# Low parts of weights on VectorE alone, and a three-tap convolution shared differently between ScalarE and VectorE

## The chip, the cores and the metric

The kernel runs on one core of a Trainium2 chip. The metric is the device time of one execution in microseconds (us). TensorE (PE in the profile) multiplies matrices, VectorE (DVE), ScalarE (ACT) and GpSimd (POOL) work element by element, and SyncE (SP) issues the transfers.

## The reference, cut to what matters

The model has two kinds of blocks, each of depth 2, on 256 tokens of 1024 channels. The first block is a SwiGLU feed-forward, a mixer (a gated spatial unit and top-k attention), a second SwiGLU feed-forward. The second block is a mixer (a gated delta rule and dilated attention) and a feed-forward with a causal convolution over three tokens:

```
def _causal_dwconv(x, w):
    K = w.shape[0]
    S = x.shape[1]
    xp = jnp.pad(x, ((0, 0), (K - 1, 0), (0, 0)))
    y = xp[:, 0:S] * w[0]
    for j in range(1, K):
        y = y + xp[:, j:j + S] * w[j]
    return y

def _conv_glu_ffn(h, ffn_up, ffn_conv, ffn_conv_bias, ffn_down):
    u = _causal_dwconv(h @ ffn_up, ffn_conv) + ffn_conv_bias
    gate, val = jnp.split(u, 2, axis=-1)
    return (jax.nn.gelu(gate, approximate=True) * val) @ ffn_down
```

All of it is fp32, and every product with a weight matrix is taken to better than the precision of one pass of TensorE.

## The kernel before

Activations lie with channels on the 128 partitions and 256 tokens along the free axis. Every weight matrix comes from HBM in slabs of 128 x 1024 fp32 (512 KB; some are 768 or 512 wide). `parts` makes two tiles of each slab: ScalarE copies `wraw` to `whi` in TensorE's rounded format, and `wlo` is the remainder, `wraw` minus `whi`. `mm3` then runs three passes over a slab: eight pairs of a product with `whi` and one with `wlo` against the high part of the activations, and eight products with `whi` against their low part, 24 matmuls of 128 x 256 for a slab of 1024. The three tiles of a slab turn over in four buffers each: the load of a new slab (issued by SyncE) waits until both readers of an old `wraw` are done, and a new `whi` or `wlo` waits until TensorE has finished the slab four back.

Before the change a low part is divided: GpSimd makes the last `pool_cols` columns (384 as a rule) and VectorE the rest. In the second mixer (`mixer2`) the plan gives 24 slabs of each layer to GpSimd whole: their entries have 1024 or no number of columns of their own, and the line with `FULL` sets it to the whole width.

The stages follow each other: for each layer `swiglu`, `mixer1`, `swiglu`; then for each layer `mixer2`, `conv_glu`. A feed-forward has 22 chunks of 128 hidden channels; a chunk takes two slabs (gate and value) and gives one PSUM bank of 128 x 512. In `conv_glu` each chunk is multiplied by the row scales (`t`), convolved (`y`: ScalarE multiplies by the last tap and adds the bias, VectorE adds the other two taps, two instructions for each half), run through Gelu (`s`), multiplied by the other half (`p`) and split into `hid`: high part on ScalarE, low part on GpSimd. The down projection then takes 22 x 24 matmuls.

In `mixer2` the program writes TensorE's order by hand: the delta rule's chain of small steps (`Delta`) runs with products of the projections between its steps as filler (`pump`). The chain begins with the decay rates on tiny tiles (`bt`, `xa`, `spe`, `spz`, `sps`, `dg`: 128 x 8 or 16), side by side with the convolution of the keys (`ct`, `kT`), all on VectorE; TensorE waits for `dg`. Later GpSimd masks `LT` and makes `dM`, and VectorE's `Tf` needs them.

Elsewhere a scheduler orders each engine's instructions when the program is built; on the chip each engine takes its own list in that order.

Of the kernel before, what the change touches and what calls it, by code (L numbers as in the profile page):

```python
# [7 lines left out]
F32 = mybir.dt.float32  # L8
R32 = mybir.dt.float32r
AF = mybir.ActivationFunctionType  # L10
OP = mybir.AluOpType
# [6 lines left out]
P = 128  # L18
T = 256
D = 1024  # L20
# [5 lines left out]
NEG = -1.0e30  # L26
TAKEN = -3.0e38
BANKS = {"mm": 3, "sm": 5}
FIRST_COLS = 384
POOL_COLS = 384  # L30
FULL = 34
X_ENG = ((ACT, ACT), (ACT, ACT))
XT_ENG = ((ACT, ACT), (ACT, ACT))
WARM = (0, 5, 3)
# [56 lines left out]
class Kernel:  # L91
# [9 lines left out]
    def run(self, stages=None):  # L101
        nc, I, cp = self.nc, self.I, self.cp
        stages = stages or STAGES
        first = [s for s in stages if s[0] not in ("final", "mixer2", "glu")]
        vec1 = self.load(cp, [P, 8 + 2 * V1], I["vec1"], "vec1")
        self.x, self.ahead = [], []
        self.before = self.latest = self.ready = self.later = None
        self.plan, self.made, self.queue, self.far = [], [], [], 0
        self.pool_cols = FIRST_COLS
        for d in range(KD):  # L110
            n = self.new_x()
            nc.sync.dma_start(n, I["x"][d])
            self.x.append(n)
            if d == 1 and stages[0] == ("ffn1", 0):
                self.ahead.append(self.raw(I["ffn1_gu"][0][0, 0], D, 2))
        if self.ahead:
            self.made.append(self.parts(None, D, 0, step=D // 2))
            self.ahead.append(self.raw(I["ffn1_gu"][0][0, 1], D))
            idle = self.sp.tile([P, T], F32, name="sq", bufs=5)
            nc.vector.memset(idle, 0.0)  # L120
            self.warm(10, idle)
        self.ident = self.load(cp, [P, P], I["ident"], "ident")
        self.ones = cp.tile([P, 1], F32, name="ones")
        nc.vector.memset(self.ones, 1.0)
        self.mhalf = cp.tile([P, 16], F32, name="mhalf")
        nc.vector.memset(self.mhalf, -0.5)
        with Pool(self.tc, name="const1", bufs=1) as cp:
            con = self.vec2 = None
            for n, (kind, l) in enumerate(first):
                if n == 1:  # L130
                    self.second_constants()
                v = vec1[:, 8 + V1 * l:8 + V1 * (l + 1)]
                if kind == "mixer1":
                    if con is None:
                        con = {n: self.load(cp, list(I[n].shape), I[n], n)
                               for n in ("cos1", "sin1", "causal0", "causal1")}
                        self.cos1, self.sin1 = con["cos1"], con["sin1"]
                        self.causal = [con["causal0"], con["causal1"]]
                    self.mixer1(l, v)
                else:  # L140
                    g = V_FFN1 if kind == "ffn1" else V_FFN2
                    self.swiglu(v[:, g:g + 8], I[kind + "_gu"][l], I[kind + "_down"][l])
        if self.vec2 is None:
            self.second_constants()
        self.pool_cols = POOL_COLS
        with Pool(self.tc, name="const2", bufs=1) as cp:
            con = {n: self.load(cp, list(I[n].shape), I[n], n)
                   for n in ("cos2", "sin2", "dil0", "dil1", "cum", "whole", "levels", "ident2")}
            self.cos2, self.sin2 = con["cos2"], con["sin2"]
            self.dilated = [con["dil0"], con["dil1"]]  # L150
            self.cum, self.whole, self.levels = con["cum"], con["whole"], con["levels"]
            self.ident2 = con["ident2"]
            rest = stages[len(first):]
            for n, (kind, l) in enumerate(rest):
                v = self.vec2[:, V2 * l:V2 * (l + 1)]
                g = None
                if n + 1 < len(rest):
                    c = V2 * rest[n + 1][1] + (V_PRE if rest[n + 1][0] == "mixer2" else V_PREF)
                    g = self.vec2[:, c:c + KD]
                if kind == "final":  # L160
                    self.between(vec1[:, :KD], g)
                elif kind == "mixer2":
                    self.mixer2(l, v, g)
                else:
                    self.conv_glu(v, I["up2"][l], I["down2"][l], g)
        for d in range(KD):
            nc.sync.dma_start(self.out[d], self.x[d])
# [52 lines left out]
            self.nc.sync.dma_start(raw[:, c:c + step], src[:, c:c + step])  # L220
        return raw

    def piece(self, src, n, pool_cols=None):

        if self.plan or self.made:
            while self.plan and len(self.made) < 3:
                self.made.append(self.parts(*self.plan.pop(0)))
            for p in self.plan[len(self.ahead):self.far]:
                self.ahead.append(self.raw(p[0], p[1]))
            return self.made.pop(0)  # L230
        return self.parts(src, n, pool_cols)

    def parts(self, src, n, pool_cols=None, tiles=None, step=None):
        nc = self.nc
        raw = self.ahead.pop(0) if self.ahead else self.raw(src, n)
        if tiles is None:
            hi = self.wp.tile([P, n], R32, name="whi", tag="whi", bufs=4)
            lo = self.wp.tile([P, n], R32, name="wlo", tag="wlo", bufs=4)
        else:
            hi, lo = tiles  # L240
        hf = hi.bitcast(F32)
        step = step or n
        for a in range(0, n, step):
            e = a + step
            self.act(hi[:, a:e], raw[:, a:e])
            c = e - min(step, self.pool_cols if pool_cols is None else pool_cols)
            if c > a:
                self.tt(lo[:, a:c], raw[:, a:c], hf[:, a:c], OP.subtract)
            if c < e:
                self.tt(lo[:, c:e], raw[:, c:e], hf[:, c:e], OP.subtract, nc.gpsimd)  # L250
        return hi, lo

    def mm3(self, ps, w, hs, start=True, stop=True, M=P):
# [271 lines left out]
    def conv_glu(self, vec, wup, wdown, following):  # L525
        nc = self.nc
# [3 lines left out]
        with Pool(self.tc, name="glu", bufs=2) as fp:  # L530
            hid = []
            for j in range(NF):
                if pss:
                    ps = pss.pop(0)
                else:
                    ps = self.bank([P, 2, T])
                    for s in range(2):
                        self.mm3(ps[:, s, :], self.piece(wup[j, s], D), hs)
                t = fp.tile([P, 2, T], F32, name="t")
                self.tt(t, ps, rb2)  # L540
                y = fp.tile([P, 2, T], F32, name="y")
                for s in range(2):
                    c = j + NF * s
                    tap = lambda i: vec[:, V_FC + 3 * c + i:V_FC + 3 * c + i + 1]
                    self.act(y[:, s, :], t[:, s, :], AF.Identity, scale=tap(2), bias=vec[:, V_FB + c:V_FB + c + 1])
                    for i in (1, 0):
                        sh = 2 - i
                        self.stt(y[:, s, sh:], t[:, s, :T - sh], tap(i), y[:, s, sh:], OP.mult, OP.add)
                a = fp.tile([P, T], F32, name="s")
                self.act(a, y[:, 0, :], AF.Gelu_apprx_tanh)  # L550
                p = fp.tile([P, T], F32, name="p")
                self.tt(p, a, y[:, 1, :])
                hid.append(self.split(fp, p, "hid", NF, nc.gpsimd))
            ys, acc = [], None
            for m in range(KD):
                ps = self.bank([P, T])
                for q in range(0, NF, KD):
                    e = min(q + KD, NF)
# [307 lines left out]
    def mixer2(self, l, vec, following):  # L866
# [3 lines left out]
        wo = I["w_out2"][l]  # L870
        half = lambda m, i: (wo[m, :, 512 * i:512 * i + 512], 512)
        first = {"q": 0, "v": 8, "z": 12, "Q": 16, "K": 20}
        self.plan = [(w[i], D, 512) for i in range(4, 8)]
        for c in ORDER:
            if c == "V":
                self.plan += [(I["w_in2_v"][l, i], D) for i in range(4)]
            else:
                self.plan += [(w[first[c] + i], D, 512 if c in "qvz" else None) for i in range(2)]
                first[c] += 2
        self.plan = [p if n < 4 or n >= 4 + FULL else p[:2] + (p[1],) for n, p in enumerate(self.plan)]  # L880
        self.plan += [half(m, 0) for m in range(KD)]
        with Pool(self.tc, name="mix2", bufs=1) as mp, self.tc.manual_schedule(engines={PE}):

# [55 lines left out]
            def tap(c, i):  # L939
                return vec[:, V_DNC + 4 * c + i:V_DNC + 4 * c + i + 1]  # L940
# [89 lines left out]
            def delta_part():  # L1030
                for m in range(KD):
                    w = self.piece(None, 0)

                    t = [mp.tile([P, 512], R32, name=n, tag="big", bufs=16) for n in ("obh", "obl")]
                    wob.append(self.parts(*half(m, 1), None, t))
                    yield from self.mm3_steps(part(m), w, oa, m % 2 == 0, False, shared=True)

            def attention_part(m, i):
# [498 lines left out]
```

## Time and profile before

| | |
|---|---|
| median of 3 runs | 2001.97 us (1999.31 to 2010.21) |
| the profiled execution | 2004.46 us, of which its span is 2002.8 us |
| busy, share of the span | PE 95%, DVE 66%, ACT 49%, POOL 61% |
| granted clock of TensorE, mean | 0.981 |

The span runs from the first to the last instruction of the profiled execution. PE's matmuls are pipelined and their ends are modelled, so a busy PE is read together with the number of matmuls in a stretch.

### The profile page before, as it was taken

To read this page: it belongs to the slowest core of one execution; us is meant where nothing else is said; L and a number is where in the kernel's file an instruction comes from. 1 tells how busy PE (TensorE), PEld (TensorE's weight loads), DVE (VectorE), ACT (ScalarE), POOL (GpSimd) and SP (SyncE) were. 2 spreads that over 40 slices of the span, in tenths; PEclk is the share of its full clock that TensorE was granted. 3 is DMA by queue.
4 is the path that set the end of the run, shared out by engine and by line. 5 is a ranking of instruction groups with operands and counts; after the bars stand their busy time and mean duration, and the time that the engine had idled before them with its cause. 6 is when DMAs were issued, how large, how long until landed. Compare 5 with 4: busy or idle time off the path is not lost. (4 is left out here: it accounts for less than half of the span.)

```text
span 2002.8 us, 40107 instructions
## 1 busy us (share of the span) xinstructions
PE 1894.3 (95%) x15468; PEld 1822.9 (91%) x15468; DVE 1321.7 (66%) x2270; ACT 988.0 (49%) x1698; POOL 1217.8 (61%) x957
## 2 busy tenths in 40 slices
PE   9999999899999999999999978999899979999988
PEld 8999889899999999899999977879888978789888
DVE  7665685866657755966776567457884484559862
ACT  5444436444445544455445534455554445455553
POOL 5556475655565665665566757565556767555555
PEclk9999999999999999999899989999999989999999
DMA  7566554555656666555566633142555332235553
GB/s 233 187 183 187 182 162 130 187 171 188 184 185 198 193 183 192 170 165 154 169 197 187 193 117 116 57 147 88 166 158 174 126 121 92 68 113 169 165 164 114
DMA packets 102511, 317.17 MB, mean 158 GB/s; under 512 B 13360, under 2 KB 20912, under 8 KB 102320
## 3 DMA queue, kind: packets, MB, share of 16 engines
q1 hardware_dynamic: 102320, 314.61, 50.1%
q8 instruction: 121, 1.98, 0.4%
q14 instruction: 70, 0.57, 0.1%
HBM read 309.58 MB, written 1.05 MB: 155 GB/s over the span
## 5 line engine op out<-in xcount | busy, mean ns | idle before, releaser
L202 POOL TENSOR_TENSOR wlo<-wraw,whi 128x384 fp32r<-128x384 f32 (+1 forms) x609 | 931.0, 1532 | 490.0 <-ACT whi L185 487.3
L263 PE MATMUL mm<-h,whi 128*128 128x256 f32 x6048 | 1085.4, 282 | 18.2 <-DVE h L374 5.2
L263 PEld LDWEIGHTS mm<-h,whi 128*128 128x128 f32 x6048 | 931.9, 190 | 29.4 <-issue 12.1
L185 ACT ACTIVATE whi<-wraw 128x1024 fp32r<-128x1024 f32 (+2 forms) x611 | 611.0, 1003 | 421.2 <-PE mm L263 125.5
L263 PE MATMUL mm<-h,wlo 128*128 128x256 f32 (+1 forms) x3024 | 731.5, 282 | 30.5 <-DVE wlo L202 24.4
L202 DVE TENSOR_TENSOR wlo<-wraw,whi 128x640 fp32r<-128x640 f32 (+3 forms) x563 | 487.8, 867 | 333.8 <-ACT whi L185 332.2
L263 PEld LDWEIGHTS mm<-h,wlo 128*128 128x128 f32 (+1 forms) x3024 | 574.8, 190 | 38.6 <-DVE wlo L202 31.6
L263 PE MATMUL mm<-hid,whi 128*128 128x256 f32 x2112 | 378.9, 282 | 6.9 <-ACT hid L185 6.1
L263 PEld LDWEIGHTS mm<-hid,whi 128*128 128x128 f32 x2112 | 326.4, 190 | 7.7 <-ACT hid L185 6.5
L263 PE MATMUL mm<-hid,wlo 128*128 128x256 f32 x1056 | 257.3, 281 | 2.9 <-DVE wlo L202 2.9
L263 PEld LDWEIGHTS mm<-hid,wlo 128*128 128x128 f32 x1056 | 199.5, 189 | 4.1 <-DVE wlo L202 4.1
L185 ACT ACTIVATE hid<-p 128x256 fp32r<-128x256 f32 x132 | 55.1, 418 | 182.9 <-DVE p L202 182.8
L205 DVE SCALAR_TENSOR_TENSOR y<-t,vec,y 128x254 f32<-128x254 f32 (+1 forms) x176 | 135.8, 828 | 0.0
L202 DVE TENSOR_TENSOR p<-s,t 128x256 f32<-128x256 f32 x88 | 103.4, 1175 | 2.2 <-ACT s L185 2.2
L202 DVE TENSOR_TENSOR t<-mm,rb 128x512 f32<-128x512 f32 x132 | 90.5, 686 | 20.4 <-PE mm L263 12.2
L202 POOL TENSOR_TENSOR hid<-p,hid 128x256 fp32r<-128x256 f32 x44 | 34.7, 789 | 88.3 <-ACT hid L185 88.3
L202 DVE TENSOR_TENSOR hid<-p,hid 128x256 fp32r<-128x256 f32 x88 | 40.7, 463 | 40.2 <-ACT hid L185 40.2
L202 POOL TENSOR_TENSOR ssum<-ssum,sq 128x256 f32<-128x256 f32 x50 | 49.0, 981 | 12.1 <-ACT sq L185 11.1
L185 ACT ACTIVATE s<-y 128x256 f32<-128x256 f32 x44 | 18.4, 417 | 69.1 <-DVE y L205 68.9
L263 PE MATMUL mm<-zh,whi 128*128 128x256 f32 x256 | 46.6, 283 | 4.6 <-DVE gate L202 1.8
L205 DVE SCALAR_TENSOR_TENSOR h<-x,vec,h 128x256 fp32r<-128x256 f32 x72 | 45.8, 644 | 6.2 <-ACT h L185 5.1
L185 ACT ACTIVATE y<-t,vec 128x256 f32<-128x256 f32 x88 | 47.5, 589 | 1.7 <-DVE t L202 1.7
(296 smaller groups left out, 2038.4 us busy)
## 6 DMA issues: line engine op xcount, KB each, us to landing
wraw<-ffn_gu_in SPq DMA_DIRECT2D x175, 512.0 KB
wraw<-w_in_a_in SPq DMA_DIRECT2D x112, 512.0 KB
wraw<-up_in SPq DMA_DIRECT2D x88, 512.0 KB
wraw<-ffn_down_in SPq DMA_DIRECT2D x64, 512.0 KB
wraw<-down_in SPq DMA_DIRECT2D x32, 512.0 KB
wraw<-ffn_down_in SPq DMA_DIRECT2D x32, 384.0 KB
wraw<-w_in_v_in SPq DMA_DIRECT2D x16, 512.0 KB
wraw<-w_out_in SPq DMA_DIRECT2D x16, 512.0 KB
```

What stands on the lines that cost most here:

```text
L185: return self.nc.scalar.activation(out, in_, func, **k)
L202: return (eng or self.nc.vector).tensor_tensor(out, a, b, op=op)
L205: return self.nc.vector.scalar_tensor_tensor(out, a, s, b, op0=op0, op1=op1)
L263: mm = lambda a, b, **f: self.nc.tensor.matmul(ps, a, b, skip_group_check=shared, **f)
```

## The change

Low parts are made by VectorE alone, in one instruction for a whole slab; the columns' counts and the plan's numbers go. In `conv_glu` ScalarE multiplies by the middle tap into a new tile `m` (one instruction for each half), VectorE still adds the first tap for each half, and one VectorE instruction adds `m`, moved by one token, to both halves.

```
-FIRST_COLS = 384
-POOL_COLS = 384
-FULL = 34
...
         for a in range(0, n, step):
             e = a + step
             self.act(hi[:, a:e], raw[:, a:e])
-            c = e - min(step, self.pool_cols if pool_cols is None else pool_cols)
-            if c > a:
-                self.tt(lo[:, a:c], raw[:, a:c], hf[:, a:c], OP.subtract)
-            if c < e:
-                self.tt(lo[:, c:e], raw[:, c:e], hf[:, c:e], OP.subtract, nc.gpsimd)
+            self.tt(lo[:, a:e], raw[:, a:e], hf[:, a:e], OP.subtract)
         return hi, lo
...
                 y = fp.tile([P, 2, T], F32, name="y")
+                m = fp.tile([P, 2, T], F32, name="m")
                 for s in range(2):
                     c = j + NF * s
                     tap = lambda i: vec[:, V_FC + 3 * c + i:V_FC + 3 * c + i + 1]
                     self.act(y[:, s, :], t[:, s, :], AF.Identity, scale=tap(2), bias=vec[:, V_FB + c:V_FB + c + 1])
-                    for i in (1, 0):
-                        sh = 2 - i
-                        self.stt(y[:, s, sh:], t[:, s, :T - sh], tap(i), y[:, s, sh:], OP.mult, OP.add)
+                    self.act(m[:, s, :], t[:, s, :], scale=tap(1))
+                    self.stt(y[:, s, 2:], t[:, s, :T - 2], tap(0), y[:, s, 2:], OP.mult, OP.add)
+                self.tt(y[:, :, 1:], y[:, :, 1:], m[:, :, :T - 1], OP.add)
...
-        self.plan = [(w[i], D, 512) for i in range(4, 8)]
+        self.plan = [(w[i], D) for i in range(4, 8)]
...
-                self.plan += [(w[first[c] + i], D, 512 if c in "qvz" else None) for i in range(2)]
+                self.plan += [(w[first[c] + i], D) for i in range(2)]
                 first[c] += 2
-        self.plan = [p if n < 4 or n >= 4 + FULL else p[:2] + (p[1],) for n, p in enumerate(self.plan)]
```

VectorE in the steady part of the up projection of `conv_glu`, one chunk, before:

```order
L205 SCALAR_TENSOR_TENSOR y<-t,vec_2479,y 128x255 x2
L205 SCALAR_TENSOR_TENSOR y<-t,vec_2479,y 128x254 x2
L202 TENSOR_TENSOR wlo<-wraw,whi 128x640
L202 TENSOR_TENSOR p<-s,y 128x256
L202 TENSOR_TENSOR t<-mm,rb 128x512
L202 TENSOR_TENSOR wlo<-wraw,whi 128x640
```

The same chunk after the change (lines have moved up by five):

```order
L200 SCALAR_TENSOR_TENSOR y<-t,vec_2412,y 128x254 x2
L197 TENSOR_TENSOR y<-y,m 128x2x255
L197 TENSOR_TENSOR wlo<-wraw,whi 128x1024
L197 TENSOR_TENSOR p<-s,y 128x256
L197 TENSOR_TENSOR t<-mm,rb 128x512
L197 TENSOR_TENSOR wlo<-wraw,whi 128x1024
```

Of the four tap instructions two stay, one addition of both halves takes the place of the other two, and the low parts are whole slabs.

ScalarE in the same chunk, before:

```order
L185 ACTIVATE whi<-wraw 128x1024
L185 ACTIVATE s<-y 128x256
L185 ACTIVATE hid<-p 128x256
L185 ACTIVATE whi<-wraw 128x1024
L185 ACTIVATE y<-t,vec_2479 128x256 x2
```

ScalarE in the same chunk, after:

```order
L180 ACTIVATE whi<-wraw 128x1024
L180 ACTIVATE s<-y 128x256
L180 ACTIVATE whi<-wraw 128x1024
L180 ACTIVATE hid<-p 128x256
L180 ACTIVATE y<-t,vec_2412 128x256
L180 ACTIVATE m<-t,vec_2412 128x256
L180 ACTIVATE y<-t,vec_2412 128x256
L180 ACTIVATE m<-t,vec_2412 128x256
```

Two multiplications by the middle tap are new, and a copy of a slab now stands between Gelu and the high part of `hid`.

VectorE at the head of the delta rule in the second layer's `mixer2`, from the first decay rates to the first tap of the keys, before:

```order
L202 TENSOR_TENSOR bt<-sm,rt 128x32
L202 TENSOR_TENSOR bt<-bt 128x2x8
L202 TENSOR_TENSOR xa<-bt,dt 128x8
L205 SCALAR_TENSOR_TENSOR spe<-xa 128x8
L999 COPY rb<-sm 128x256
L202 TENSOR_TENSOR ct<-mm,rb 128x512
L1139 TENSOR_SCALAR spz<-spe 128x8
L1141 RECIPROCAL spz<-spz 128x8
L205 SCALAR_TENSOR_TENSOR kT<-ct,vec_2479,kT 128x255
```

The same place after the change:

```order
L197 TENSOR_TENSOR xa<-bt,dt 128x8
L197 TENSOR_TENSOR wlo<-wraw,whi 128x1024
L200 SCALAR_TENSOR_TENSOR spe<-xa 128x8
L989 COPY rb<-sm 128x256
L197 TENSOR_TENSOR wlo<-wraw,whi 128x1024
L197 TENSOR_TENSOR ct<-mm,rb 128x512
L197 TENSOR_TENSOR wlo<-wraw,whi 128x1024
L1129 TENSOR_SCALAR spz<-spe 128x8
L197 TENSOR_TENSOR wlo<-wraw,whi 128x1024
L1131 RECIPROCAL spz<-spz 128x8
L200 SCALAR_TENSOR_TENSOR kT<-ct,vec_2412,kT 128x255
L197 TENSOR_TENSOR wlo<-wraw,whi 128x1024
```

Five low parts that GpSimd made stand here among the decay rates, and a sixth follows before `dg`; in the first layer there are six as well. TensorE's own order of instructions is the same before and after.

## Rows read from the trace of the kernel before

**Rows 1.** The page's chain that ended last, by line.

```profile
PE mm L263 9%; DVE y L205 5%; DVE wlo L202 2%; ACT whi L185 2%; DVE p L202 1%; POOL wlo L202 1%; PE sm L1262 1%; PE sm L336 1%; POOL x L202 1%; PE sm L1388 1%; PE sm L1272 0%; ACT as L185 0%; PE sm L1387 0%; PE sm L263 0%; POOL ssum L202 0%
```

**Rows 2.** Stretches: length, busy (count) of PE, PEld, DVE, ACT, POOL; PEclk, DMA, GB/s.

```profile
589.79:710.63 120.84, 120.84 (x1067) 120.84 (x1067) 86.22 (x111) 60.25 (x88) 71.80 (x46) 1.00 0.61 191
...
1153.72:1362.94 209.22, 184.76 (x1460) 166.86 (x1458) 121.82 (x278) 97.42 (x236) 127.46 (x107) 0.95 0.32 104
1362.94:1517.00 154.06, 138.26 (x1151) 133.77 (x1151) 131.67 (x193) 90.56 (x151) 89.37 (x77) 1.00 0.47 149
...
1578.26:1782.50 204.24, 185.70 (x1459) 168.32 (x1459) 122.98 (x278) 100.40 (x247) 132.21 (x113) 0.96 0.30 98
1782.50:1936.00 153.50, 138.51 (x1150) 134.30 (x1150) 131.33 (x193) 90.36 (x151) 89.09 (x76) 1.00 0.46 150
```

**Rows 3.** Timeline of VectorE, one chunk of `conv_glu`: start, duration, instruction, [idle before].

```profile
1445.44 0.41 DVE L202 TENSOR_TENSOR p<-s,y 128x256 f32<-128x256 f32 x1
1445.77 0.68 DVE L202 TENSOR_TENSOR t<-mm,rb 128x512 f32<-128x512 f32 x1
1447.29 0.83 DVE L202 TENSOR_TENSOR wlo<-wraw,whi 128x640 fp32r<-128x640 f32 x1 [0.84 <-ACT whi L185]
1448.03 3.19 DVE L205 SCALAR_TENSOR_TENSOR y<-t,vec,y 128x255 f32<-128x255 f32 x4
1451.15 0.81 DVE L202 TENSOR_TENSOR wlo<-wraw,whi 128x640 fp32r<-128x640 f32 x1
1451.88 0.41 DVE L202 TENSOR_TENSOR p<-s,y 128x256 f32<-128x256 f32 x1
```

**Rows 4.** Timeline of ScalarE, the same chunk.

```profile
1445.88 0.42 ACT L185 ACTIVATE hid<-p 128x256 fp32r<-128x256 f32 x1 [0.98 <-DVE p L202]
1446.21 1.05 ACT L185 ACTIVATE whi<-wraw 128x1024 fp32r<-128x1024 f32 x1
1447.16 1.08 ACT L185 ACTIVATE y<-t,vec 128x256 f32<-128x256 f32 x2
1448.14 1.05 ACT L185 ACTIVATE whi<-wraw 128x1024 fp32r<-128x1024 f32 x1
```

**Rows 5.** Timeline of TensorE, the next chunk's first product with the low part.

```profile
1452.02 0.38 PE L263 MATMUL mm<-h,wlo 128*128 128x256 f32 x1 [0.72 <-DVE wlo L202]
```

**Rows 6.** Timeline of GpSimd, the same chunk's low part of `hid`.

```profile
1452.83 0.74 POOL L202 TENSOR_TENSOR hid<-p,hid 128x256 fp32r<-128x256 f32 x1 [2.27 <-ACT hid L185]
```

**Rows 7.** Timeline of VectorE at the head of the second layer's `mixer2`.

```profile
1593.81 2.08 DVE L202 TENSOR_TENSOR bt<-bt 128x16 f32<-128x16 f32 x1
...
1605.31 2.63 DVE L205 SCALAR_TENSOR_TENSOR kT<-ct,vec,kT 128x255 f32<-128x255 f32 x1
...
1608.14 0.48 DVE L205 SCALAR_TENSOR_TENSOR kT<-ct,vec,kT 128x254 f32<-128x254 f32 x1
...
1611.43 0.16 DVE L205 SCALAR_TENSOR_TENSOR dg<-sps,ea 128x8 f32<-128x8 f32 x1
```

**Rows 8.** Timeline of GpSimd in the same place.

```profile
1598.11 9.55 POOL L202 TENSOR_TENSOR wlo<-wraw,whi 128x1024 fp32r<-128x1024 f32 x4
```

**Rows 9.** TensorE's waits in the first layer's `mixer2`: total, times, longest.

```profile
PE sm L1171 <- DVE dg L205: 9.8, 1, 9.8
PE sm L1264 <- POOL LT L1244: 5.7, 1, 5.7
PE mm L263 <- POOL wlo L202: 2.6, 2, 2.1
```

**Rows 10.** TensorE's waits in the second layer's `mixer2`.

```profile
PE sm L1171 <- DVE dg L205: 7.5, 1, 7.5
PE sm L1274 <- DVE Tf L202: 3.5, 2, 3.2
PE mm L263 <- POOL wlo L202: 3.4, 3, 2.1
```

**Rows 11.** Groups by line and shape: low parts of whole slabs on GpSimd.

```profile
L202 POOL TENSOR_TENSOR wlo<-wraw,whi 128x1024 fp32r<-128x1024 f32 x48 | 116.3, 2435 | 61.6 <-ACT whi L185 61.5
```

More of the change, by code (lines that the diff above doesn't have):

```diff
@@ L108, in run @@
         self.plan, self.made, self.queue, self.far = [], [], [], 0
-        self.pool_cols = FIRST_COLS
         for d in range(KD):
@@ L116, in run @@
         if self.ahead:
-            self.made.append(self.parts(None, D, 0, step=D // 2))
+            self.made.append(self.parts(None, D, step=D // 2))
             self.ahead.append(self.raw(I["ffn1_gu"][0][0, 1], D))
@@ L144, in run @@
             self.second_constants()
-        self.pool_cols = POOL_COLS
         with Pool(self.tc, name="const2", bufs=1) as cp:
@@ L221, in raw, with piece @@
         return raw
-    def piece(self, src, n, pool_cols=None):
+    def piece(self, src, n):
         if self.plan or self.made:
@@ L230, in piece, with parts @@
             return self.made.pop(0)
-        return self.parts(src, n, pool_cols)
-    def parts(self, src, n, pool_cols=None, tiles=None, step=None):
-        nc = self.nc
+        return self.parts(src, n)
+    def parts(self, src, n, tiles=None, step=None):
         raw = self.ahead.pop(0) if self.ahead else self.raw(src, n)
@@ L1034, in delta_part @@
                     t = [mp.tile([P, 512], R32, name=n, tag="big", bufs=16) for n in ("obh", "obl")]
-                    wob.append(self.parts(*half(m, 1), None, t))
+                    wob.append(self.parts(*half(m, 1), t))
                     yield from self.mm3_steps(part(m), w, oa, m % 2 == 0, False, shared=True)
```

## The prediction

> **What bounds the kernel now.** I first read the chain that ended last. TensorE holds the largest share, and the largest share of another engine is VectorE's taps of the convolution, 5% of the span, with low parts and the copies of slabs behind them [rows 1]. So I looked for the stages in which TensorE does not run at its own pace. That pace comes from an up projection of `swiglu`: 1067 matmuls in 120.84 us with PE busy throughout, 0.1133 us each [rows 2]. There the weights, the low parts and the transfers keep up. A chunk of two slabs, 48 matmuls, needs 5.44 us at this pace.
>
> The up projection of `conv_glu` is slower. Its stretch takes 154.06 us with 1151 matmuls, which need 130.4 us, so 23.7 us are lost; in the second layer it is 153.50 us for 1150, 23.2 us lost [rows 2]. The timeline of VectorE shows why: from one `p` to the next, 1445.44 to 1451.88, is 6.44 us [rows 3]. The parts form a ring over two engines. `p` releases the high part of `hid` on ScalarE, behind it in ScalarE's list stands the copy of a slab, VectorE waits 0.84 us for this copy, makes a low part, runs the four taps (3.1 us), makes the other low part, and only then comes the next `p` [rows 3, 4]. TensorE meets the ring's end as a wait of 0.72 us for a low part, once a chunk [rows 5].
>
> The second place is `mixer2`, 209.22 and 204.24 us [rows 2]. Its largest waits of TensorE are those for `dg`, 9.8 and 7.5 us, then for the masked `LT` (5.7) or `Tf` (3.5) and for low parts of GpSimd (2.6 and 3.4) [rows 9, 10].
>
> **The price of VectorE's instructions.** The spacing of starts counts, since an instruction begins a little before the last has ended. A low part of 640 columns is spaced 0.74 us and `p` of 256 0.33 us [rows 3]. That is 1.07 ns a column, so a low part of 1024 is an estimated 1.15 us, and an instruction of 512, such as `t`, or of 510, such as the new addition, 0.60 us. A tap that nothing holds lasts 0.48 us [rows 7] and is spaced 0.40; in the steady chunk the four take 3.12 us, 0.78 each [rows 3]. The difference is GpSimd at work on low parts.
>
> **The change in `conv_glu`.** VectorE's list for a chunk is then 2 x 1.15 (low parts) + 0.60 (`t`) + 2 x 0.40 (first taps) + 0.60 (the addition) + 0.33 (`p`) = 4.63 us. GpSimd keeps one instruction per chunk, the low part of `hid`, 0.74 us [rows 6]; if it holds VectorE for all of that each time, 5.37. ScalarE's list is 2 x 0.95 (slabs), 0.98 (both `y`), at most 0.98 (both `m`, which have a scale and no bias) and 2 x 0.33 (`s` and the high part of `hid`), 4.52 us [rows 4]. All stay below 5.44. The ring opens as well: the copy no longer stands behind the high part of `hid`. What is left of it, from one addition to the next, is a low part 1.15, `p` 0.33, `t` 0.60, then ScalarE's four multiplications 1.96 and the addition with its hand-overs 0.65: 4.7 us. So TensorE should set the pace, with `t` waiting for it. Low parts are made about two chunks ahead and the buffers of `whi` come free at TensorE's pace, as they already do in `swiglu`, so its waits for them should go. The transfers are those of the fast stretch, which asked for 191 GB/s [rows 2].
>
> I leave 3 us of the loss at the head of each stage, where TensorE waits for the norm, and take 20.5 us a layer, **41 us** in all. Bounds: all of it, 47; and 22 if hand-overs and GpSimd's instruction keep a chunk at 5.9 us, since half of the 1.00 us per chunk is then lost again.
>
> **The change in `mixer2`.** At its head five of VectorE's small instructions, from `bt` to the second tap of the keys, last 2.08 to 2.63 us, 11.6 us together [rows 7]; unhindered, tiny ones take 0.16 and taps 0.48 [rows 7], 1.4 us together. The other 10.1 us are spent while GpSimd makes low parts, four of them in 9.55 us [rows 8], 2.44 each in the mean [rows 11].
>
> The Trainium skill, SBUF — State Buffer, section "Who interferes with whom", says that a VectorE instruction with two SBUF inputs and a GpSimd instruction that reads SBUF exclude each other, and that the later one blocks until the other has ended. By that rule the whole 10.1 us is blocking and goes with GpSimd's low parts, as in my sum; if the engines merely shared bandwidth, sixteen elements could hardly last 2.08 us and part of it would stay. The trace agrees with the rule.
>
> Against it stand six low parts that VectorE now makes ahead of `dg`, 6 x 1.15 = 6.9 us. The balance is 3.2 us; some of the new work falls into VectorE's waits for ScalarE, and the first layer has one more held instruction, so I take 4 us a layer, **8 us**. Bounds: nothing, if the low parts wait for ScalarE's copies in the middle of the chain, and 11.
>
> The waits for `LT`, `Tf` and GpSimd's low parts sum to 15.2 us [rows 9, 10]. GpSimd is then free when the mask comes. But TensorE's own order asks for the low parts of two more slabs before it turns `LT`, and VectorE makes them only behind its eight instructions for `LT`. I estimate a new wait of 2.5 us a layer from two such low parts (2 x 1.15), and take 15.2 - 5 = **10 us**. Bounds: 0 and 15.
>
> VectorE has room: in each `mixer2` it is busy 122 of over 204 us [rows 2], stalls included, and gains 24 low parts, 28 us, and the rest of the halved slabs of the output projection, some 6 us.
>
> **The clock.** In both `mixer2` stretches the granted clock is 0.95 and 0.96 in the mean, against 1.00 in the others shown [rows 2]; it is at 1.2 GHz for a part of them, after TensorE's long waits. At 209.22 and 204.24 us that is 10.5 and 8.2 us of lost clock. Shorter waits should return about a third, **6 us**; bounds 0 and 12.
>
> **Everything else.** `swiglu` is at TensorE's pace already; VectorE's list for its chunk, about 3.6 us by the prices above, is still below 5.44, so nothing comes or goes. At the joints, where VectorE makes norms and low parts by turns, blocking by GpSimd goes and wider low parts come; the first mixer has both too. I take **3 us** gain, bounds -8 and +8.
>
> **The sum.** 41 + 8 + 10 + 6 + 3 = 68 us. The profiled execution took 2004.46 us, 1.66 more than its span of 2002.8, and lies 2.49 above the median of 2001.97. 2002.8 - 68 = 1934.8, plus 1.66 is 1936.5; against the median of the runs, **1934 us**.
>
> **Rivals.**
> 1. `conv_glu` comes only to 5.9 us a chunk, by VectorE, GpSimd's `hid` and the hand-overs together. For it: 5.37 of 5.44 leaves little. Against it: `t` waits for TensorE anyway and GpSimd's work falls mostly there. It costs 19 us: 1953. Chance 10%.
> 2. `mixer2` gives nothing: low parts in front of the decay rates and of `Tf` cost what the blocking cost. For it: VectorE's list is one queue, and a low part that waits for ScalarE's copy, which waits for TensorE, holds all behind it. Then 8 + 10 + 6 us are not gained: 1958. Chance 10%. The Trainium skill, TensorE: Matmul & The Clock Gate, section "Architectural detail", says that VectorE takes its instructions strictly in order; no run here shows it yet with a low part at the front.
> 3. Slower than before: in each `mixer2` all that VectorE gains in work, 34 us, lands on the chain that TensorE waits for, and as much blocking is hidden as was before. That is +68 against 44 gained elsewhere: 2026. It decides when a `mixer2` grows by more than 22 us. Against it: VectorE is idle there for 80 us. Chance 3%.
> 4. The change does not do its work in `conv_glu`: ScalarE, with two multiplications more and copies that wait for TensorE to free a buffer, becomes the ring, and a chunk stays at 6.4. Only 27 us come: 1975. Against it: 4.52 us of work. Chance 3%.
>
> The forecast has the other 74%.
>
> **How the numbers follow.** The forecast's own range, with its terms' bounds combined, is 1912 to 1955. The 8-in-10 range takes in rivals 1 and 2 with their own spread and the case that all upper bounds come: 1910 to 1966. A measurement of this kernel can tell 0.5%, 10 us, from no change; below 1992 lie the forecast and rivals 1, 2 and 4. Faster 0.95, same 0.02, slower 0.03.
>
> **What would show it.** Right: spacing of `p` in `conv_glu` near 5.44 us and TensorE's wait for a low part gone there; taps at 0.48 us, low parts of 1024 at about 1.21; the small instructions before `dg` at 0.2 us or less, and waits for `dg` of 4 to 6 us; no wait for `LT` over 3 us. Wrong: a low part of 1024 far above 1.2 us, ScalarE idle in front of copies while VectorE waits behind them, or a wait of TensorE for VectorE in `mixer2` that is longer than before [rows 9, 10].

## The result and the profile after

The median is 1944.81 us (1940.72 to 1945.77, 4 runs), against 2003.73 us (1999.31 to 2010.21, 4 runs) of the kernel before on the same chip: a ratio of 0.970, with a 95% interval of 0.9668 to 0.9731. The forecast was 1934 us, with 1910 to 1966 as its range; the time came out 11 us above the one and inside the other. The profiled execution took 1945.77 us, its span is 1944.0 us.

The page's chain that ended last, by line, after the change (against [rows 1]):

```profile
PE mm L253 10%; PE sm L618 0%; PE sm L1378 0%; PE sm L1262 0%; PE sm L253 0%; PE mm L574 0%; PE sm L326 0%; PE sm L1377 0%; DVE yo L197 0%; PE sm L637 0%; PE mm L576 0%; PE mm L575 0%; POOL ssum L197 0%; PE sm L651 0%; POOL x L197 0%
```

The chain is followed back only to 1631.92 us here, so the two lists cover different stretches. Where it runs, from the second layer's `mixer2` on, it holds no tap of the convolution, two low parts and three copies of slabs, all in `mixer2`, and no line of another engine than TensorE reaches 1%.

Stretches of the kernel after, in the order of [rows 2]: `mixer2` and the up projection of `conv_glu`, first and second layer.

```profile
1144.27:1352.19 207.92, 187.18 (x1461) 168.95 (x1459) 126.97 (x303) 98.39 (x236) 48.06 (x61) 0.96 0.32 103
1352.19:1478.16 125.97, 124.88 (x1081) 124.45 (x1082) 115.43 (x164) 102.96 (x185) 37.98 (x30) 0.99 0.54 174
1544.94:1744.72 199.78, 185.98 (x1458) 168.72 (x1459) 126.81 (x302) 102.25 (x247) 57.53 (x69) 0.96 0.31 99
1744.72:1870.62 125.90, 124.83 (x1081) 124.39 (x1082) 115.49 (x164) 103.00 (x185) 38.01 (x30) 0.99 0.55 174
```

`mixer2` took 209.22 and 204.24 us before and hardly became shorter: 1.3 and 4.5 us. Where the gain lies is seen when the program is cut at the first matmul of each stage (the first that reads `h`, `hid` or `oa`, and the first of the attention's output) and the lengths are compared. The first row of `mixer2` is called its first part below. Cut so, the up projection before ends at 1502.57 us, and the last 14.4 us of the stretch of 154.06 us in [rows 2] already belong to the down projection.

| us from TensorE's first matmul of the stage to the next (the last one to VectorE's last instruction) | before | after | difference |
|---|---|---|---|
| six stages of the first block together | 1148.15 | 1138.44 | -9.7 |
| `mixer2`, to the output of the delta rule | 165.88, 161.25 | 159.27, 152.17 | -6.6, -9.1 |
| `mixer2`, attention's stretch | 23.95, 23.60 | 28.86, 28.11 | +4.9, +4.5 |
| `mixer2`, output and norm | 19.39, 19.39 | 19.79, 19.50 | +0.4, +0.1 |
| `conv_glu`, up projection | 139.63, 139.25 | 125.97, 125.90 | -13.7, -13.4 |
| `conv_glu`, down projection | 75.69, 78.14 | 66.78, 70.56 | -8.9, -7.6 |

VectorE in the steady part of `conv_glu`, one chunk (against [rows 3]):

```profile
1433.10 0.69 DVE L197 TENSOR_TENSOR y<-y,m 128x510 f32<-128x510 f32 x1
1433.71 1.22 DVE L197 TENSOR_TENSOR wlo<-wraw,whi 128x1024 fp32r<-128x1024 f32 x1
1434.84 0.42 DVE L197 TENSOR_TENSOR p<-s,y 128x256 f32<-128x256 f32 x1
1435.18 0.69 DVE L197 TENSOR_TENSOR t<-mm,rb 128x512 f32<-128x512 f32 x1
1435.93 1.23 DVE L197 TENSOR_TENSOR wlo<-wraw,whi 128x1024 fp32r<-128x1024 f32 x1
1437.08 1.36 DVE L200 SCALAR_TENSOR_TENSOR y<-t,vec,y 128x254 f32<-128x254 f32 x2
...
1440.28 0.42 DVE L197 TENSOR_TENSOR p<-s,y 128x256 f32<-128x256 f32 x1
```

From one `p` to the next is 5.44 us, to the hundredth the pace taken for TensorE; it was 6.44. ScalarE now waits for TensorE to free a buffer of `whi`, which says the same:

```profile
1434.84 1.07 ACT L180 ACTIVATE whi<-wraw 128x1024 fp32r<-128x1024 f32 x1 [0.59 <-PE mm L253]
```

GpSimd's one instruction in the chunk (against [rows 6]) became longer, 1.48 us instead of 0.74:

```profile
1436.28 1.48 POOL L197 TENSOR_TENSOR hid<-p,hid 128x256 fp32r<-128x256 f32 x1 [3.96 <-ACT hid L180]
```

It begins beside VectorE's low part of 1435.93 and ends at 1437.76. The first of the two taps, alone, lasts 0.96 us, twice the 0.48 of a free one [rows 7], and the second 0.47:

```profile
1437.08 0.96 DVE L200 SCALAR_TENSOR_TENSOR y<-t,vec,y 128x254 f32<-128x254 f32 x1
```

VectorE at the head of the second layer's `mixer2` (against [rows 7]):

```profile
1559.55 0.17 DVE L197 TENSOR_TENSOR bt<-bt 128x16 f32<-128x16 f32 x1
1559.76 0.17 DVE L197 TENSOR_TENSOR xa<-bt,dt 128x8 f32<-128x8 f32 x1
1559.85 1.22 DVE L197 TENSOR_TENSOR wlo<-wraw,whi 128x1024 fp32r<-128x1024 f32 x1
...
1568.00 0.48 DVE L200 SCALAR_TENSOR_TENSOR kT<-ct,vec,kT 128x255 f32<-128x255 f32 x1
```

The tiny instructions shown last 0.17 us instead of 2.08 and a tap 0.48 instead of 2.63, with low parts of 1.22 us between them. TensorE's waits in `mixer2` (against [rows 9, 10]), first layer:

```profile
PE sm L1161 <- DVE dg L200: 5.1, 1, 5.1
PE mm L253 <- DVE wlo L197: 4.5, 2, 3.7
PE sm L637 <- POOL as L197: 3.5, 1, 3.5
PE sm L1262 <- DVE Tf L197: 2.3, 5, 0.8
PE sm L1264 <- DVE Tf L197: 1.5, 2, 1.3
```

and second layer:

```profile
PE sm L1161 <- DVE dg L200: 5.4, 1, 5.4
PE sm L637 <- POOL as L197: 3.4, 1, 3.4
...
PE sm L1264 <- DVE Tf L197: 1.7, 2, 1.5
PE sm L1262 <- DVE Tf L197: 1.0, 3, 0.4
```

The waits for `LT` and for GpSimd's low parts are gone. New are a wait for a low part of VectorE (first layer only) and one for `as`, the probabilities of the attention, which was 0.2 us before in the first layer. The waits for `Tf` became longer in the first layer (3.8 us, 0.8 before). The low part of the first layer's longest wait, 3.7 us, stands in VectorE's list behind instructions on `x`, which finish the stage before:

```profile
1208.66 2.81 DVE L200 SCALAR_TENSOR_TENSOR x<-x,vec,sm 128x256 f32<-128x256 f32 x7
...
1212.07 1.21 DVE L197 TENSOR_TENSOR wlo<-wraw,whi 128x1024 fp32r<-128x1024 f32 x1
```

The wait for `as` has to do with ScalarE's order; runs 3 and 4 show how much. ScalarE at the start of the attention, before:

```profile
1320.38 1.28 ACT L185 ACT_TABLE_LOAD   x1
1322.92 0.51 ACT L185 ACTIVATE as<-as,ast 128x256 f32<-128x256 f32 x1 [1.26 <-DVE ast L631]
```

and after:

```profile
1306.80 0.64 ACT L180 ACTIVATE obh<-wraw 128x512 fp32r<-128x512 f32 x1 [2.21 <-DMA wraw<-w_out_in]
...
1309.29 0.64 ACT L180 ACTIVATE whi<-wraw 128x512 fp32r<-128x512 f32 x1 [1.32 <-issue]
1309.94 1.28 ACT L180 ACT_TABLE_LOAD   x1
1311.23 0.51 ACT L180 ACTIVATE as<-as,ast 128x256 f32<-128x256 f32 x1
```

Before, the load of the table for the exponential was done 1.26 us ahead of the scores. After, two more copies of slabs (and one more `obh`) stand in front of it. A copy lasts 0.6 us, but ScalarE stands idle ahead of them, 2.21 us until a slab's transfer has landed and 1.32 us more. So the load begins only at 1309.94, when VectorE had already written the maxima, `ast`, at 1308.77.

### The profile page after: what moved, and what is told of

It is laid out like the page before. It is cut to its first block, busy times and chain, and to the rows that moved or that the text cites. A ratio compares the mean times of both kernels' runs of the same rounds, so it can differ in the third digit from the quotient of the medians.

```text
span 1944.0 us, 38985 instructions
## 1 busy us (share of the span) xinstructions
PE 1880.5 (97%) x15468; PEld 1820.5 (94%) x15468; DVE 1336.7 (69%) x2274; ACT 1026.8 (53%) x1786; POOL 323.3 (17%) x332
## 5 line engine op out<-in xcount | busy, mean ns | idle before, releaser
L197 DVE TENSOR_TENSOR wlo<-wraw,whi 128x1024 fp32r<-128x1024 f32 (+2 forms) x611 | 715.8, 1174 | 370.9 <-ACT whi L180 368.6
L253 PE MATMUL mm<-hid,whi 128*128 128x256 f32 x2112 | 374.1, 279 | 0.0
L197 POOL TENSOR_TENSOR ssum<-sq 128x256 f32<-128x256 f32 x19 | 23.3, 1231 | 662.7 <-ACT sq L180 662.7
L197 POOL TENSOR_TENSOR hid<-p,hid 128x256 fp32r<-128x256 f32 x44 | 64.6, 1470 | 178.9 <-ACT hid L180 147.5
L197 POOL TENSOR_TENSOR ssum<-ssum,sq 128x256 f32<-128x256 f32 x50 | 54.9, 1099 | 203.9 <-ACT sq L180 178.4
L200 DVE SCALAR_TENSOR_TENSOR y<-t,vec,y 128x254 f32<-128x254 f32 x88 | 53.9, 652 | 0.3 <-ACT y L180 0.3
L197 POOL TENSOR_TENSOR as<-as,ast 128x512 f32<-128x512 f32 (+1 forms) x32 | 26.4, 827 | 124.4 <-DVE ast L626 94.9
L200 DVE SCALAR_TENSOR_TENSOR h<-x,vec,h 128x256 fp32r<-128x256 f32 x72 | 41.1, 578 | 6.0 <-ACT h L180 5.1
L180 ACT ACTIVATE m<-t,vec 128x256 f32<-128x256 f32 x88 | 43.3, 496 | 1.8 <-DVE t L197 1.8
L253 PEld LDWEIGHTS mm<-zh,whi 128*128 128x128 f32 x256 | 39.0, 188 | 2.4 <-ACT zh L180 2.4
```

What stands on the lines that cost most here:

```text
L180: return self.nc.scalar.activation(out, in_, func, **k)
L197: return (eng or self.nc.vector).tensor_tensor(out, a, b, op=op)
L200: return self.nc.vector.scalar_tensor_tensor(out, a, s, b, op0=op0, op1=op1)
L253: mm = lambda a, b, **f: self.nc.tensor.matmul(ps, a, b, skip_group_check=shared, **f)
```

## The experiments

Each time is a median, with the ratio to the kernel before on the same chip (2006.59, 2005.35 and 2005.23 us in the three groups of runs, in this order).

**1. The convolution alone.** The kernel before, with only the lines of `conv_glu` changed as in the change.

> The kernel before with the change's convolution alone; GpSimd keeps its share of the low parts. Theory (GpSimd's low parts hold VectorE, and both parts of the change are needed): the remaining taps still last about 0.8 us each and the addition over 1 us, so a chunk of conv_glu comes from 6.44 only to 5.7 to 6.0 us, the two up projections give back 20 to 30 of the 43.6 us, the rest of the kernel stays as before: about 1977 us. Rival (fewer instructions on VectorE are enough): a chunk at 5.44 us, both stages as after the change, about 1960 us. Under a second rival (the new convolution is worth nothing while GpSimd holds VectorE) a chunk stays above 6.2 us, 1995 us or more.

1974.56 us, 0.9839 (0.9817 to 0.986). One chunk on VectorE, and GpSimd beside it:

```profile
1441.01 1.25 DVE L202 TENSOR_TENSOR p<-s,y 128x256 f32<-128x256 f32 x1
...
1443.75 1.35 DVE L205 SCALAR_TENSOR_TENSOR y<-t,vec,y 128x254 f32<-128x254 f32 x2
...
1446.55 1.25 DVE L202 TENSOR_TENSOR p<-s,y 128x256 f32<-128x256 f32 x1
```
```profile
1440.29 2.84 POOL L202 TENSOR_TENSOR wlo<-wraw,whi 128x384 fp32r<-128x384 f32 x2 [1.40 <-ACT whi L185]
```

`p` lasts 1.25 us, held by GpSimd, where a free one lasts 0.42. Still the chunk is at 5.54 us, between the theory's 5.7 and the rival's 5.44. The up projection takes 125.97 us in the first layer, as after the whole change, and 128.65 in the second (at the slower pace of TensorE that run 5 shows). The 0.1 us by which a chunk is late is met by TensorE at the start of the first layer's down projection, as a wait of 2.8 us for `hid`, and the down projections keep 71.58 and 71.59 us. So for the up projection the rival is right. Run 1 gained 32 of the 59 us; the others are not the convolution's alone.

**2. The low parts alone.** The kernel after, with the four old taps.

```
-                    self.act(m[:, s, :], t[:, s, :], scale=tap(1))
-                    self.stt(y[:, s, 2:], t[:, s, :T - 2], tap(0), y[:, s, 2:], OP.mult, OP.add)
-                self.tt(y[:, :, 1:], y[:, :, 1:], m[:, :, :T - 1], OP.add)
+                    for i in (1, 0):
+                        sh = 2 - i
+                        self.stt(y[:, s, sh:], t[:, s, :T - sh], tap(i), y[:, s, sh:], OP.mult, OP.add)
```

> The kernel after with the old four taps on VectorE and no middle tap on ScalarE; VectorE alone makes the low parts. Theory (the taps were slow because GpSimd worked on low parts): taps spaced 0.40 us, VectorE's list 2 x 1.15 + 0.60 + 4 x 0.40 + 0.33 = 4.83 us for a chunk, 5.57 with GpSimd's low part of hid in the way, so a chunk at 5.44 to 5.6 us and 1945 to 1952 us in all. Rival (four taps in series behind a copy are the ring, held or not): a chunk at 5.9 us or more, that is 1964 us or more.

1946.06 us, 0.9694 (0.9673 to 0.9716): as fast as the whole change. VectorE:

```profile
1433.95 2.15 DVE L200 SCALAR_TENSOR_TENSOR y<-t,vec,y 128x255 f32<-128x255 f32 x4
...
1437.15 0.41 DVE L197 TENSOR_TENSOR p<-s,y 128x256 f32<-128x256 f32 x1
```

Four taps take 2.15 us instead of 3.19 [rows 3], and the first layer's up projection is 125.95 us. The theory held in the main: the taps were slow because GpSimd made low parts beside them. They are not all at 0.40 us: the first of the four still lasts 0.96, beside GpSimd's low part of `hid`. The new convolution adds nothing that can be measured to this.

**3. The output projection's halves shared with GpSimd again.** The kernel after, with

```
+            c = e - 384 if n == 512 and self.second else e
-            self.tt(lo[:, a:e], raw[:, a:e], hf[:, a:e], OP.subtract)
+            self.tt(lo[:, a:c], raw[:, a:c], hf[:, a:c], OP.subtract)
+            if c < e:
+                self.tt(lo[:, c:e], raw[:, c:e], hf[:, c:e], OP.subtract, self.nc.gpsimd)
```

where `second` is set for the second block.

> The kernel after, but the low parts of the halved slabs of mixer2's output projection are divided again as before (128 columns on VectorE, 384 on GpSimd). With it ScalarE's order at the start of the attention is that of before: the table load and the first exponentials stand ahead of the copies that came before them after the change. Theory: the wait of 3.5 and 3.4 us for the probabilities goes, the stretch from the delta rule's output to the attention's output returns from 28.9 and 28.1 to about 24 us, together 8 to 9 us less: 1936 us. Rival (GpSimd's low parts block VectorE's reductions and its own probabilities, or the dips of the clock stay): no gain, 1943 us or more.

1938.56 us, 0.9654 (0.9613 to 0.9694). The attention's stretches are 23.99 and 23.72 us and the longest wait for the probabilities is 0.4 us in both layers, in the first:

```profile
PE sm L642 <- POOL as L199: 0.7, 2, 0.4
```

The stretches bear the theory out. The total does so less sharply: two of the four runs took 1943 and 1944 us, where the rival puts them.

**4. The first exponential ahead of the copies.** The kernel after, VectorE making all low parts; only ScalarE's order is held (an instruction in the block is queued behind the first exponential; this kernel is version 4 below):

```
+                    hold = lambda n: self.tc.issue_after(self.exp.ins) if m >= n else nullcontext()
+                    with hold(2):
-                    w = self.piece(None, 0)
+                        w = self.piece(None, 0)
...
+                    with hold(3):
-                    wob.append(self.parts(*half(m, 1), t))
+                        wob.append(self.parts(*half(m, 1), t))
```

> The kernel after with one thing moved: on ScalarE the copies of the output projection's slabs from the fifth on stand behind the first exponential of the attention, so that the table load comes earlier; VectorE makes all low parts. Theory (ScalarE's order alone makes the new wait): the wait for the probabilities falls from 3.5 us to 1 us or less, the attention's stretch to 24 or 25 us in both layers, 1936 to 1938 us. Rival (VectorE's 512-wide low parts between the scores make it): the wait stays at 2.5 us or more and the time at 1943 us or more.

1933.76 us, 0.9634 (0.9613 to 0.9655). The attention's stretches are 23.03 and 22.58 us, but a shorter wait stays, in the first layer:

```profile
PE sm L639 <- POOL as L198: 2.1, 2, 1.6
```

Before its first exponential ScalarE now waits for VectorE (idle 2.37 us, ended by `ast`). So ScalarE's order makes about half of the 3.5 us, between theory (1 or less) and rival (2.5 or more). The rest goes when the low parts are divided as well (0.4 us in run 10). The stretch is shorter than the theory's 24 to 25 us, and the output behind it 1.4 and 3.5 us longer. With the waits went dips of the granted clock, that is stretches at 1.2 instead of 2.4 GHz: after the change TensorE's clock was at 1.2 GHz for 6.83 us, beginning within each wait for `as`, an estimated 3.4 us lost in each attention. Here no dip falls into the attention's stretch, and one of 3.41 us into the second layer's output.

**5. The kernel after, once more.**

> The kernel after once more, for the spread between profiled executions of one program. Theory (stages whose work did not change differ between programs for reasons that repeat): each stage within 0.5 us of the first profile, once half of the time at 1.2 GHz is taken off; about 1945 us. Rival (the dips of the clock fall at random): stages with a dip differ by 1.7 to 5 us, and the first six stages cannot be compared from single profiles.

1947.48 us, 0.9716 (0.9694 to 0.9738). Not only dips differ between two profiles of one program. Two stretches of 40 us of this one execution, in the up projections of the first and of the second layer:

```profile
1430.00:1470.00 40.00, 40.00 (x355) 40.00 (x354) 38.66 (x53) 33.31 (x60) 10.54 (x8) 1.00 0.61 195
1800.00:1840.00 40.00, 40.00 (x342) 40.00 (x341) 37.63 (x51) 32.22 (x58) 10.65 (x7) 1.00 0.58 186
```

TensorE is busy throughout at a granted clock of 1.00 and waits for nobody, but runs 355 matmuls in the one and 342 in the other: they are spaced 113.3 and 117.8 ns, a chunk of 48 takes 5.44 or 5.65 us, and a stretch without waits holds one pace or the other to its end. The rival held, with a second kind of difference. To compare single profiles I therefore take from a stage's length half of its time at 1.2 GHz and 4.4 ns for each matmul spaced 117 to 119 ns. That is an estimate: where TensorE waits during a dip, half is too much. What is left, from the first matmul to VectorE's last instruction, is 1870.7 us in both profiles of the kernel after (single stages still differ by up to 1.6 us) and 1926.2 before: 55.5 us less work; the dips gave 6.8 us more (35.8 us lost before, 29.0 after) and the slower pace took 3.3 (32.3 and 35.6). 55.5 + 6.8 - 3.3 = 59.0 us is the difference of the two profiles.

**6. mixer2's slabs on GpSimd as before.**

```
+        self.plan = [p if n < 4 else p + (None, None, True) for n, p in enumerate(self.plan)]
...
-            self.tt(lo[:, a:e], raw[:, a:e], hf[:, a:e], OP.subtract)
+            self.tt(lo[:, a:e], raw[:, a:e], hf[:, a:e], OP.subtract, self.nc.gpsimd if pool else None)
```

> The kernel after, but in both mixer2 the low parts of the 24 slabs behind the first four are made whole by GpSimd, as before. Theory (GpSimd's low parts held the small instructions at the head and the masking of LT): small instructions before dg last over 2 us again, TensorE's wait for dg returns from 5.1 and 5.4 to 7 to 10 us, that for LT or Tf to 3 us or more, and the first parts of mixer2 grow from 159.3 and 152.2 us to about 165 and 160: together 10 to 15 us, 1955 to 1960 us. Rival (what VectorE gained was lost again by its own low parts ahead of dg and Tf, and the first part became shorter for other reasons, clock or order): less than 4 us, 1949 us or less.

1955.33 us, 0.976 (0.9735 to 0.9785). The first parts are 165.94 and 158.14 us. Without clock and pace they are 154.8 and 152.0, as before the change (155.0 and 152.0), against 153.5 and 145.9 after it. So of the work the low parts make 1.3 us in the first layer and 6.1 in the second. The old waits are back in the first layer:

```profile
PE sm L1162 <- DVE dg L200: 9.7, 1, 9.7
PE sm L1255 <- POOL LT L1235: 5.9, 1, 5.9
...
PE mm L253 <- POOL wlo L197: 2.4, 2, 2.1
```

In the second they are 7.1 us for `dg`, 4.1 for low parts and 2.0 for `Tf` (3.5 before). At its head:

```profile
1564.30 2.39 DVE L197 TENSOR_TENSOR xa<-bt,dt 128x8 f32<-128x8 f32 x1
...
1573.60 2.65 DVE L200 SCALAR_TENSOR_TENSOR kT<-ct,vec,kT 128x255 f32<-128x255 f32 x1
```

Eight elements a partition take 2.39 us beside a low part of GpSimd, and 0.17 without. That is the theory, undone and seen to return.

**7. The first block's low parts divided as before**, 384 columns of each slab on GpSimd in `swiglu` and `mixer1` (the same lines as in 3, with `c = e if self.second else e - min(step, 384)`).

> The kernel after, but in the first block (swiglu and mixer1, both layers) the low parts are divided as before, 384 columns on GpSimd. Theory (the 11.5 us that the first six stages gave come from the low parts): they return, the first six stages take 1148 us instead of 1138, 1953 to 1957 us. Rival (they are dips of the clock that fell elsewhere): 1943 to 1948 us, with no stage longer by over 2 us once the clock's share is taken off.

1961.54 us, 0.977 (0.9737 to 0.9803). Without clock and pace the six stages take 1109.2 us, against 1101.3 and 1101.6 in the two profiles of the kernel after and 1113.4 before. The joints, where one stage passes into the next, show where: TensorE's waits at the start of the second `swiglu` are back in both layers, in the second as before (1.8 and 1.5 us there),

```profile
PE mm L258 <- DVE wlo L199: 1.9, 1, 1.9
PE mm L258 <- DVE h L369: 1.5, 1, 1.5
```

and after the change they are one wait of 0.5 us in the second layer and none in the first. So some 8 of the 12 us of work are shown to be the low parts'; the other 4 stay open. The time itself, 1961.54 us, is above the theory's 1953 to 1957; its profile lost 5.1 us more to dips and 4.2 more to the slower pace than the first one of the kernel after.

**8. More work for VectorE**, one instruction in each chunk of `conv_glu`:

```
+                again = fp.tile([P, 2, T], F32, name="again")
+                self.tt(again, t, rb2)
```

> The kernel after with one more VectorE instruction of 128x512 in each chunk of conv_glu (t times the row scales into a tile that nothing reads; it is pure extra work). It measures how much room VectorE has. Theory (VectorE's list of 4.63 us is what counts; GpSimd's low part of hid waits for VectorE and not the other way): 5.23 us, a chunk stays at 5.44 to 5.5 us, the time grows by less than 4 us. Rival (GpSimd's instruction holds VectorE for its whole length, so that the chunk has no room left): 5.97 us a chunk, some 0.5 us more for each of 44, the time grows by 20 to 25 us to 1967 us or so.

1941.38 us (1933.16 to 1953.67), 0.9682 (0.9632 to 0.9732): no slower. VectorE even waits for TensorE once a chunk, in the first layer:

```profile
1427.93 0.69 DVE L197 TENSOR_TENSOR t<-mm,rb 128x512 f32<-128x512 f32 x1 [0.37 <-PE mm L253]
```

The chunk there is 5.65 us (TensorE's slower pace), of which VectorE fills 5.28: the list of 4.63, the 0.60 added, and 0.05. In the second layer TensorE has the faster pace, 5.44 us a chunk, and VectorE still waits for it; the up projection takes 125.89 us there, 125.90 without the added work:

```profile
1848.98 0.69 DVE L197 TENSOR_TENSOR t<-mm,rb 128x512 f32<-128x512 f32 x1 [0.15 <-PE mm L253]
1849.59 0.87 DVE L200 SCALAR_TENSOR_TENSOR y<-t,vec,y 128x254 f32<-128x254 f32 x2
```

So the theory held for the time: there is room for the added instruction. Its second half, that GpSimd's instruction waits and VectorE's never does, did not hold for the kernel after: there the two taps take 1.36 us, here 0.87.

**9. More filler ahead of `dg`.** Version 4 with `WAIT["ba"]` at 10.3 instead of 5.8.

> The kernel with the first exponential ahead of the copies, and 4.5 us more of projection work (10.3 instead of 5.8) pumped into TensorE's order before it turns to the rates that dg ends. Theory (dg is late by VectorE's chain alone, so TensorE can take work from later there): the wait for dg falls from 5.1 and 5.4 us to about 2, the first parts of mixer2 become 3 us shorter each, about 6 us in all. Rival (the two more slabs need two more low parts of VectorE ahead of dg, 1.15 us each, and the work taken is missing later, at the levels of the inverse): no gain, the first parts within 1.5 us of 159.0 and 153.0.

1938.72 us, 0.9659 (0.9625 to 0.9694). The wait for `dg` fell to 1.6 and 2.1 us, but another took its place in both layers:

```profile
PE sm L1403 <- POOL do L198: 4.5, 1, 4.5
```

The place fits the rival, work moved forward that is missing behind the scan, where GpSimd scales `do`; that this is the reason was not tested. The first part was 155.57 us in the first layer and 156.50 in the second, 3.4 us less and 3.5 more than in version 4. Each layer settles by its own balance; half of the theory and half of the rival.

**10. Both remedies of the attention.**

> Both remedies of the attention's wait together: the first exponential ahead of the copies, and the halved slabs' low parts divided with GpSimd. Theory (the wait has two parts, ScalarE's order and VectorE's low parts): no wait for the probabilities above 0.5 us, the attention's stretch 23 to 24 us and the output's 20 us, 2 to 3 us less than with either alone. Rival (each alone takes all that there is): 1933 to 1939 us, as with either.

1937.64 us, 0.9674 (0.9637 to 0.971): nothing beyond either alone, as the rival said. The waits went as the theory said: the longest for the probabilities is 0.4 us, the stretches are 23.9 and 23.7 us, the output 20.0 in both layers.

**11. Version 4 again**, beside 9 and 10.

> The kernel with the first exponential ahead of the copies once more, beside the two other versions on one chip, to settle which is best: 1934 us, attention's stretches of 23 us and 22.6 us again, with or without a dip of the clock behind them.

1934.92 us, 0.966 (0.963 to 0.969), with attention's stretches of 22.76 and 22.58 us. Twice about 1934 us against 1945 and 1947 of the change: version 4 is the best found, though the kernels of runs 3, 9 and 10 cannot be told from it by their intervals.

## Why the prediction was right, and where its terms were off

- **conv_glu, 41 us: measured 43.5** (27.0 in the up projections, 16.5 in the down projections). The chunk came to 5.44 us, VectorE's list to 4.68 where nothing holds it (run 8, less the 0.60 added; 4.63 as summed), and TensorE's wait for a low part went. The place was read wrong: the stretch of 154.06 us reached 14.4 us into the down projection, so the loss of 23.7 us was not the up projection's alone. The attribution was off too: the step costed both edits as parts of one sum, but run 2 gives the same with the low parts alone, and run 1 gives the up projection with the convolution alone. They are two ways to open one ring, not two gains. Rival 1 fell with run 8: the room was at least 0.6 us a chunk, not 0.07. GpSimd's low part of `hid` does hold VectorE, one tap for 0.49 us a chunk, though not for 0.74, and it is itself held by a low part (0.74 became 1.48); the sign "taps at 0.48 us" came true for one of the two taps. Rival 4 did not happen: ScalarE waits for TensorE.
- **mixer2's head, 8 us, and the waits for `LT`, `Tf` and low parts, 10 us: the mechanism right, the sizes too large.** The waits for `dg` fell by 4.7 and 2.1 us, 6.8 together. Of the others, I had allowed a new wait of 2.5 us in each layer; it was 4.5 in the first, with 3.8 for `Tf` where 0.8 had been, and in the second nearly nothing. The waits of both layers for `LT`, `Tf` and low parts, VectorE's included, fell from 16.3 to 11.3 us, 5 where 10 had been summed, and the wait of 3.7 us for a low part is one of the prediction's own signs of being wrong. In the first layer the missed low part stands in VectorE's list behind `LT` and behind seven instructions on `x` that finish the stage before and two of the rotation; the sum had counted only those for `LT`. Both first parts together became 15.7 us shorter, of which an estimated 8.5 are the clock's. The small instructions at the head had been held by GpSimd, as run 6 shows (2.39 us against 0.17). By the Trainium skill, SBUF — State Buffer, section "Who interferes with whom", the later of the two blocks until the other has ended. The trace of run 6 agrees: a low part of GpSimd lasts 2.42 us there in the mean.
- **The step that failed: what else moves in `mixer2`.** The change of the output projection's halves was counted as VectorE's work only ("some 6 us"), beside the words that VectorE has room. It moved ScalarE's table load behind more copies, which waited for their slabs, and put low parts among the scores; the attention lost 9.4 us, some 6.8 of them in dips of the clock. Runs 3 and 4 take it back. With it `mixer2` gave 5.8 us instead of 18 and its clock, and the time lies near rival 2 in that stage (nothing from `mixer2`), but not by rival 2's mechanism alone.
- **The clock, 6 us:** in `mixer2`'s first parts it gave 8.5 us, in the attentions it took 6.8, by the estimate of run 5; 1.7 in sum.
- **Everything else, 3 us: measured 9.7 over the six first stages**, outside the bound of 8. Without clock and pace it is 12 us, of which the low parts make 8 (run 7): blocking at the joints was worth more than the 3 us.
- So the total came within 11 us in part by luck, by errors of opposite sign: `mixer2` with its clock 18 us too high, and 9 us given back by `conv_glu` and the first block; the 2 us left are the kernel before, whose median was 2003.73 in this comparison and 2001.97 in the runs that the forecast started from. Rival 3 (slower) needed a `mixer2` longer by 22 us; none became longer.

## What to carry to other kernels

Two edits that open the same ring must not be summed: ask what each would leave if the other were not made. When work moves to another engine and a scheduler writes the lists, compare the new order of every engine, not only of the two concerned, above all where a table load or a long copy can slip ahead of the first step of a dependent chain. And compare stages of single profiles only after taking off the clock's dips and TensorE's pace, or by repeated runs.

## What was not expected of the hardware

TensorE has two paces at a granted clock of 1.00. The starts of the same 128x256 products lie 113.3 or 117.8 ns apart, for a whole projection, in the same program and even in two layers of one execution (355 against 342 in 40 us, run 5). Without a dip of the clock the up projection took 124.4 us at the first (both layers of run 3) and 128.7 at the second (second layer of run 1); the second layer's first `swiglu` had the faster pace in all profiles but that of run 1, and down projections always the slower. My pace of 0.1133 us came from a stage that has the faster one. Beside it, the Trainium skill, TensorE: Matmul & The Clock Gate, section "Wait — 56ns, not 53.3ns?", puts the spacing at the columns over 2.4 GHz and some 2.5 ns, which for 256 columns would be an estimated 109 ns. No long stretch here reaches it, where each product has a weight load of its own, and the rows decide. What chooses the pace was not found.
